# V times probabilities: column-tiled float32 pairs become full-array float32r matmuls of split parts

## The chip, the core and the metric

The kernel runs on one core of one Trainium2 chip. TensorE (PE) does the matrix products, and its weight loads stand in the profile as an engine of their own (PEld). VectorE (DVE), ScalarE (ACT) and GpSimd (POOL) do the elementwise work; SyncE (SP) issues the DMA transfers. Products land in PSUM, which has eight banks of 512 float32 columns for 128 partitions. All else is in SBUF or DRAM. The metric is device time in microseconds of the whole program, the median of a few executions.

## The reference, cut to what matters

Two transformer layers work on 512 latent tokens (a grid 64 wide) and 256 context tokens of 1,024 features. Layer 0 mixes tokens by neighbourhood attention with 16 heads of 64. Layer 1 mixes them by sliding-window attention in blocks of 128 queries, with 16 query heads over 4 key/value heads. Latent queries take one softmax over local keys and all context keys:

```python
s = jnp.concatenate([s_loc, s_ctx, s_sink], axis=-1)
p = jax.nn.softmax(s, axis=-1).astype(v.dtype)
return (jnp.einsum('bkgqs,bskd->bqkgd', p[..., :3 * T], v_blk)
        + jnp.einsum('bkgqc,bckd->bqkgd', p[..., 3 * T:3 * T + C], vc))
```

Each token mixer is followed by an output projection and a squared-ReLU MLP with 4,096 hidden features. Everything is float32. The last line above, V times probabilities, is what the change rewrites.

## The kernel before, in words

**Precision.** Most products run as float32r, a float32 form that TensorE takes in one pass but that keeps fewer bits. To get float32 accuracy an operand x is split into xH (x cast to float32r) and xL (x minus xH, again float32r); `split` (line 203) does this with a cast on ACT and a subtraction on DVE or POOL. A projection is then the three products H·H, H·L, L·H. Scores stack [kH; kL] over the 128 rows of the array and take [qH; qH] and [qL; qL] as stationary operands (`scores`, line 551), so that two products give all four parts. V times P is the exception: it runs in plain float32, with V (128 keys x 64 features) stationary in one half of the array's columns. `mm_halves` (line 198) puts two such products of two key blocks side by side, each into one half of the partitions of its sum, and `merge` (line 562) adds the halves with a copy on ACT and an addition on DVE.

**A head.** For each block of 128 queries PE forms the scores, DVE adds bias or mask and finds the maximum (one custom instruction), ACT takes the exponential with its sum, DVE the reciprocal, and DVE or POOL scales P. PE transposes P by blocks of 128 x 128 into PSUM (`tr`, `trs`), `evac_pt` (line 556) copies them to SBUF, and `mm_halves` takes them as moving operand.

**Layer 0.** `head0` (line 577) is one head, `qkv0(p)` (line 473) the projection of a pair of heads. `weave` (line 351) emits the steps of the attention of pair p and the projection of pair p+1 at an even pace. In `qkv0`, `front` takes a token tile's sum out of PSUM, norms it and makes `nat`; `back` transposes `nat` one tile later. In the first pairs the products of the modulation vectors (`ada_pe`) run along.

**Layer 1.** `kv1` (line 1131) projects keys, values and the first four heads' queries. `Head1` (line 1212) is one head: `front` for scores and softmax, `back` for V times P of the head before it. `q1` (line 1197) projects the next four heads' queries alongside. A query block of the two inner ones has five key blocks; its scores lie in a bank of 512 columns and in 128 columns of bank 2, so DVE takes two custom instructions in a chain. The MLPs (`mlp`, line 852) come behind each attention.

**Banks.** `banks[0..7]` are eight arrays of one PSUM bank each. In layer 0 the scores use banks 0 and 1 (`p_sc`), transposes 2, 3 and 6 (`p_pt`), V times P bank 7 (`p_pv`), projections bank 4. At the start `ada01(q)` (line 773) forms modulation vectors for two feature tiles in bank q mod 2, and `qkv0(0)` sums into banks 2 to 7. In the MLP of layer 1 the first product uses banks 4, 5, 0, 1 and the second one 2, 3, 6, 7.

**What sets the order.** Each engine runs its instructions in one fixed order. A scheduler chooses that order at build time from the program's order and its own estimate of times, and puts in the semaphore waits, so that an order can change at places that the diff does not touch. Where an engine is named in `pin`, it keeps the order of the program; PE is pinned from the MLP of layer 0 to the end of `kv1`.

Of the kernel before, what the change touches and what calls it, by code (L numbers as in the profile page):

```python
# [9 lines left out]
F32 = mybir.dt.float32  # L10
# [21 lines left out]
# column and shape of the small inputs in their pack  # L32
# [4 lines left out]
class Ring:  # L37
    """Equal slots of an arena, handed out in turn."""
# [10 lines left out]
def build(nc, tc, a):  # L49
    """a: DRAM access patterns by name."""  # L50
    with ExitStack() as es:
        _build(nc, tc, a, es)


def _build(nc, tc, a, es):
    pin = set()

    def pinned(*names):
        """Adds to `pin`; returns what undoes it."""
        added = set(names) - pin  # L60
# [53 lines left out]
    banks = [psum.tile([128, 512], F32, name=f"pq{i}", tag=f"pq{i}")[:] for i in range(8)]  # L114
# [28 lines left out]
    # the small inputs, packed  # L143
# [21 lines left out]
    # silu(c), silu(c_ctx), padded to 32 columns  # L165
# [32 lines left out]
    def mm_halves(pairs, start=False, stop=False):  # L198
        """Two products [128 x 64] . mv at once, one into each half of the partitions of its sum."""
        for at, (out, st, mv) in zip((0, 64), pairs):  # L200
            pe.matmul(out[at : at + 64], st, mv, start=start, stop=stop, tile_position=(0, at))

    def split(H_, L_, x, eng=None):
        """x == H_ + L_, both of float32r."""
# [56 lines left out]
    def ada_pe(layer, kinds, ring, ps_of, depth):  # L261
        """Vectors of the six, for both streams; one step per k tile, whose load runs `depth` steps ahead."""
# [44 lines left out]
    class Stream:  # L307
        """Weights [128, 1024] in the order of their use: loads and splits run ahead of the products."""
# [5 lines left out]
        def fill(self, n):  # L314
            """Up to n splits beyond the ones taken."""
# [18 lines left out]
    def run(gen, n=None):  # L334
        """The next n steps of a generator, or all."""
# [15 lines left out]
    def weave(*gens):  # L351
        """Generators with their step counts, emitted at an even pace."""
# [9 lines left out]
    class Stats:  # L362
        """R = 1 / sqrt(mean of squares + eps) of n tokens, on every partition; one step per feature tile."""
# [22 lines left out]
    def modulate(h_of, R, A, sh, uH, uL, tmp, view=None, split_of=None, fs=range(KT)):  # L386
        """u = h * R * A + sh, split."""
# [23 lines left out]
    def bias_tables():  # L411
        """Relative position bias per head in DRAM: of the interior queries with the mask, of the edge queries."""
# [7 lines left out]
    raw = Ring(FA, FX, 768, 2)  # L420
    xr = Ring(FA, FX + 1536, 256, 2)
    Pr = Ring(FA, FX + 2048, 512, 6)
    otmp = fr(5120, 512)
    biasr = Ring(FA, FX + 5632, 768, 2)
    natr = Ring(FA, FX + 7168, 512, 3)
# [8 lines left out]
    def head_norm(x, sq, nh):  # L434
        """rstd per head of x [128, nh * 64]; sq is scratch. One Newton step after the table functions."""
# [11 lines left out]
    def dup_mult(nat, x, r, nh, eng=g):  # L447
        """nat[:, h, 2, 64] = x[:, h, 64] * r[:, h], twice."""
# [977 lines left out]
```

## Time and profile before

| | |
|---|---|
| median of 3 runs | 1726.14 us (1725.89 to 1730.58) |
| profiled execution, first to last instruction | 1729.3 us, granted TensorE clock 0.984 of full speed |
| PE busy | 1664.0 us, 96% |
| DVE busy | 1147.3 us, 66% |
| ACT busy | 808.3 us, 47% |
| POOL busy | 568.8 us, 33% |
| chain that ended last | 73% PE, 11% DVE, 6% POOL |

The stages by their place in the profiled execution: start 0 to 75 us, attention of layer 0 to 466 us, output projection and MLP of layer 0 to 1130 us, `kv1` to 1172 us, attention of layer 1 to 1346 us, output projection and MLP of layer 1 to the end. A group row gives: line, engine, operation, out<-in by the program's names, the shape, the count | busy us, mean ns of one | idle time before, and what ended it. A timeline row gives start, length, engine, operation and how many like instructions follow each other. `pq` is PSUM; `RA` and `FA` are arenas of SBUF; `R` is one more SBUF region that is handed out anew from stage to stage. Every line number is that of a helper (L74), so names and shapes tell the groups apart. `128*64` in front of a shape is a stationary operand of 128 rows and 64 columns. A matmul's length reaches into the next one, since matmuls are pipelined; what one costs in a stream is the distance from start to start. A float32 matmul stands as two records.

### The profile page before, as it was taken

What the parts mean: (1) busy time and instruction counts of PE and PEld (TensorE: products, weight loads), DVE (VectorE), ACT (ScalarE), POOL (GpSimd) and SP (SyncE); (2) the same over time, 40 slices, a digit from 0 to 9 for tenths busy, and PEclk for the clock granted to TensorE, in tenths of its full rate; (3) what the DMA queues carried; (4) which work ended last, traced back from release to release, by engine and by line L of the source; (5) the groups of instructions that cost most, each with busy time, mean ns of one, the idle gap of its engine ahead of it and who ended that gap; (6) DMA issues with size and microseconds to landing.
All of it is one profiled execution on the core that took longest, in us unless ns stands there. A gap on an engine that the chain in (4) does not pass through costs nothing.

```text
span 1729.3 us, 25192 instructions
## 1 busy us (share of the span) xinstructions
PE 1664.0 (96%) x9554; PEld 1367.6 (79%) x9554; DVE 1147.3 (66%) x2188; ACT 808.3 (47%) x1668; POOL 568.8 (33%) x377
## 2 busy tenths in 40 slices
PE   6899999999998999999999999899999999999999
PEld 3867788887787887888888888687766988888887
DVE  5866667777467655666565656888787775555554
ACT  3656666677445343434343313556676442222220
POOL 2211111112147755749184901366551040000000
PEclk8999999999998999999999999999999999999999
DMA  9554321113124233333233311110021243232201
GB/s 312 159 179 134 121 77 45 44 52 109 38 94 155 101 114 106 128 106 122 87 119 110 122 49 62 55 44 25 13 78 63 86 158 98 97 98 96 95 30 49
DMA packets 63514, 165.63 MB, mean 96 GB/s; under 512 B 6816, under 2 KB 24608, under 8 KB 63008
## 3 DMA queue, kind: packets, MB, share of 16 engines
q1 hardware_dynamic: 63392, 164.02, 28.8%
q8 instruction: 75, 1.23, 0.3%
q14 instruction: 47, 0.39, 0.1%
HBM read 159.79 MB, written 7.34 MB: 97 GB/s over the span
## 4 chain that ended last, share of the span: by engine, by line
PE 73%; DVE 11%; POOL 6%; issue 5%; ACT 3%; DMA 2%; SPq 0%; POOLq 0%; DVEq 0%; ACTq 0%
PE pq L74 73%; DVE FA L74 5%; DVE RA L74 4%; POOL R L74 3%; POOL FA L74 2%; DMA FA<-in_ada_w_dram 2%; DVE smalls L74 2%; ACT RA L74 1%; ACT FA L74 1%; DVE R L74 1%; ACT R L74 0%; SPq L74 0%; DMA FA<-in_w_dram 0%; POOL RA L74 0%; ACT smalls L74 0%
## 5 line engine op out<-in xcount | busy, mean ns | idle before, releaser
L74 PE MATMUL pq<-RA 128*128 128x512 f32 (+3 forms) x6784 | 1282.2, 344 | 32.4 <-DVE FA L74 13.6
L74 PEld LDWEIGHTS pq<-RA 128*128 128x128 f32 x6784 | 1092.6, 192 | 193.6 <-issue 20.1
L74 ACT CAST RA<-FA 128x1024 fp32r<-128x1024 f32 (+3 forms) x299 | 230.6, 795 | 395.0 <-PE pq L74 233.8
L74 DVE TENSOR_TENSOR RA<-FA,RA 128x1024 fp32r<-128x1024 f32 (+3 forms) x265 | 300.4, 1149 | 114.2 <-ACT RA L74 109.8
L74 DVE SCALAR_TENSOR_TENSOR FA<-pq,mods,FA 128x512 f32<-128x512 f32 (+1 forms) x413 | 266.3, 662 | 159.2 <-PE pq L74 157.7
L74 POOL TENSOR_TENSOR R<-R,FA 128x1024 f32<-128x1024 f32 x84 | 221.0, 2663 | 3.8 <-ACT FA L74 1.8
L74 POOL TENSOR_TENSOR FA<-FA,smalls 128x256 f32<-128x256 f32 (+1 forms) x108 | 94.8, 880 | 362.0 <-DVE smalls L74 319.4
L74 PE MATMUL pq<-RA,R 128*128 128x512 f32 (+1 forms) x870 | 177.3, 350 | 0.6 <-DVE FA L74 0.3
L74 PEld LDWEIGHTS pq<-RA,R 128*128 128x128 f32 x870 | 143.4, 188 | 25.5 <-DVE FA L74 1.2
L74 POOL TENSOR_TENSOR FA<-FA 128x256 f32<-128x256 f32 (+2 forms) x103 | 86.5, 854 | 192.4 <-ACT FA L74 178.3
L74 PEld LDWEIGHTS pq<-ident,FA 128*128 128x128 f32 x802 | 92.4, 141 | 65.9 <-issue 49.1
L74 PE MATMUL pq<-ident,FA 128*128 128x128 f32 x802 | 134.3, 282 | 8.5 <-DVE RA L74 5.3
L74 POOL TENSOR_SCALAR FA<-FA,s 128x1024 f32<-128x1024 f32 x24 | 79.6, 3318 | 156.1 <-DMA FA<-in_ada_w_dram 127.6
L74 PE MATMUL pq<-R 128*64 128x512 f32 (+2 forms) x448 | 116.2, 471 | 3.1 <-ACT R L74 1.8
L74 ACT COPY R<-pq 128x512 f32<-128x512 f32 (+3 forms) x200 | 91.3, 476 | 40.9 <-PE pq L74 40.0
L74 POOL TENSOR_TENSOR RA<-FA,RA 128x1024 fp32r<-128x1024 f32 (+2 forms) x34 | 70.3, 2083 | 109.8 <-ACT RA L74 100.7
L74 ACT ACTIVATE FA<-FA,smalls 128x512 f32<-128x512 f32 (+1 forms) x120 | 89.2, 744 | 35.9 <-DVE smalls L74 35.0
L74 ACT ACTIVATE FA<-FA,s 128x1024 f32<-128x1024 f32 x60 | 69.0, 1151 | 78.5 <-POOL FA L74 62.7
L74 DVE SCALAR_TENSOR_TENSOR FA<-pq,FA 128x512 f32<-128x512 f32 (+1 forms) x96 | 57.1, 595 | 64.5 <-ACT FA L74 64.3
L74 ACT COPY FA<-pq 128x256 f32<-128x256 f32 (+4 forms) x130 | 55.8, 429 | 76.8 <-PE pq L74 70.9
L74 ACT ACTIVATE FA<-pq 128x512 f32<-128x512 f32 (+1 forms) x96 | 49.8, 520 | 83.2 <-PE pq L74 83.2
L74 ACT ACTIVATE FA<-FA 128x256 f32<-128x256 f32 (+1 forms) x131 | 59.2, 457 | 42.0 <-DVE FA L74 32.9
(78 smaller groups left out, 985.2 us busy)
## 6 DMA issues: line engine op xcount, KB each, us to landing
FA<-in_w_dram SPq DMA_DIRECT2D x128, 512.0 KB, 3.7
FA<-in_ada_w_dram SPq DMA_DIRECT2D x80, 512.0 KB, 3.8
FA<-in_wqkv_dram SPq DMA_DIRECT2D x32, 384.0 KB, 3.6
FA<-in_wo_dram SPq DMA_DIRECT2D x16, 512.0 KB, 3.5
FA<-in_ada_w_dram SPq DMA_DIRECT2D x20, 256.0 KB, 7.6
FA<-in_wq_dram SPq DMA_DIRECT2D x8, 512.0 KB, 3.5
R<-in_ada_w_dram SPq DMA_DIRECT2D x12, 256.0 KB, 6.2
FA<-in_xT_dram SPq DMA_DIRECT2D x2, 1024.0 KB, 6.3
```

The lines of the kernel that those rows point to most:

```text
L74: i = f(*args, **kw)
```

## The change

1. **V is split.** `front` of `qkv0` copies the whole projected tile (384 columns) to SBUF on ACT, and POOL makes vH and vL from it; `kv_front` in layer 1 does it with ACT and DVE out of PSUM. V is stored as [vH | vL], 128 columns. In layer 0 the norm factor of k is now multiplied in by POOL, no longer by DVE.
2. **P is split.** `evac_pt` writes P's transpose as H (cast on ACT) and L (subtraction on DVE).
3. **The products.** `mm_halves` goes; `pv` does two full-array float32r products for a key block, [vH | vL] with H and with L. `merge` stays: the lower half of the sum is now vL's share. The products of a block come one step later than before, behind the next block's transposes. The sum of context queries moves from bank 7 to the transposes' banks.
4. **Keys.** `key_at` puts the context's keys first, so that context and local keys of a query block are reached by one access pattern of two runs (`two`). Scores become one product of 512 keys in place of two of 256. The mask and the bias tiles follow the new key order.
5. **A two-bank array.** Banks 1 and 2 are now one array of 1,024 columns (`wide`), still handed out as two banks. In layer 1 the inner blocks' 640 scores lie in it, and DVE takes them in one custom instruction; the outer blocks use bank 0 alone.
6. **Balance and room.** In layer 1 the scaling of P of block 1 moves from DVE to ACT. The buffers of P's transposes are 3 of 1,024 (were 5 of 512) in layer 0 and 4 of 1,024 (were 3 of 512) in layer 1. The first half of `wo0` uses other weight slots.

```diff
-    banks = [psum.tile([128, 512], F32, name=f"pq{i}", tag=f"pq{i}")[:] for i in range(8)]
+    wide = None
+    banks = []
+    for i in (0, 1, 3, 4, 5, 6, 7):
+        n = 1024 if i == 1 else 512
+        x = psum.tile([128, n], F32, name=f"pq{i}", tag=f"pq{i}")
+        banks += [x[:, o : o + 512] for o in range(0, n, 512)]
+        if i == 1:
+            wide = x
...
+    def two(x, at, n):
+        x = x[:, 0:n]
+        return type(x)(x.tensor, x.offset, [list(x.ap[0]), [at, 2], [1, n]])
+    key_at = lambda t: (t + 2) % 6 * 128
...
-            s.copy(x, ps[:, 0:256])
+            s.copy(x, ps)
             V = views0(p)[3]
-            s.copy(V[:, t], ps[:, 256:384].rearrange("p (h d) -> p h d", h=2))
+            xv = x[:, 256:384].rearrange("p (h d) -> p h d", h=2)
+            g.tensor_copy(V[:, t, :, 0:DH], xv)
+            g.tensor_tensor(out=V[:, t, :, DH:128], in0=xv, in1=V[:, t, :, 0:DH].bitcast(F32), op=ALU.subtract)
...
-            v.tensor_tensor(out=nat[:, 256:384].rearrange("p (h d) -> p h d", h=2), in0=x[:, 128:256]...
+            g.tensor_tensor(out=nat[:, 256:384].rearrange("p (h d) -> p h d", h=2), in0=x[:, 128:256]...
...
-    def evac_pt(ps, lo, hi, eng=s):
+    def evac_pt(ps, lo, hi):
         pt = PTr.next()
-        (v.tensor_copy if eng is v else s.copy)(pt[:, 0 : hi - lo], ps[:, lo:hi])
-        return pt
+        H_, L_ = pt[:, 0 : hi - lo], pt[:, 512 : 512 + hi - lo]
+        s.copy(H_, ps[:, lo:hi])
+        v.tensor_tensor(out=L_, in0=ps[:, lo:hi], in1=H_.bitcast(F32), op=ALU.subtract)
+        return H_, L_
+    def pv(out, V, pt, lo, hi, start=False, stop=False):
+        for i, x in enumerate(pt):
+            mm(out, V, x[:, lo:hi], start and i == 0, stop and i == 1)
...
-                scores(ps[:, 0:256], T1, T2, t * 128, K[:, (t - 1) * 128 : (t + 1) * 128])
-                scores(ps[:, 256:512], T1, T2, t * 128, Kc)
+                scores(ps, T1, T2, t * 128, two(K, key_at(t - 1), 256))
...
     def kv_front(ps, t):
-        s.copy(V1[:, t], ps[:, 256:512].rearrange("p (h d) -> p h d", h=4))
+        xv = ps[:, 256:512].rearrange("p (h d) -> p h d", h=4)
+        s.copy(V1[:, t, :, 0:DH], xv)
+        v.tensor_tensor(out=V1[:, t, :, DH:128], in0=xv, in1=V1[:, t, :, 0:DH].bitcast(F32), op=ALU.subtract)
...
+                ps = wide[:, 0:640] if inner else p_sc.next()
+                scores(ps[:, 0:512], T1, T2, q0, two(K, key_at(first), 256))
                 if inner:
-                    px = banks[2][:, 128 * (t - 1) : 128 * t]
-                    scores(px, T1, T2, q0, K[:, q0 + 128 : q0 + 256])
-                    n1 = small()
-                    v.tensor_tensor_reduce(out=P[t][:, 512:640], in0=px, in1=mask[:, 512:640], ...)
+                    scores(ps[:, 512:640], T1, T2, q0, K[:, key_at(t + 1) : key_at(t + 1) + 128])
...
+                        elif t == 1:
+                            s.activation(P[t], P[t], AF.Copy, scale=r)
```

How the instructions stand on an engine before and now, at three places. `ISA` is the custom instruction or the reading of its accumulator; the buffer numbers of the two builds differ: before, pq_69 to pq_76 are banks 0 to 7; now pq_69 is bank 0, pq_70 is banks 1 and 2 together, and pq_71 to pq_75 are banks 3 to 7.

PE at the start, before: the modulation products of feature tiles 2 and 3 (`ada01(1)`, pq_70) stand ahead of the first products of `qkv0(0)` (pq_71 and on).

```order
L74 MATMUL pq_69<-FA,s_97 32x128 x12
L74 MATMUL pq_70<-FA,s_97 32x128 x4
L74 MATMUL pq_69<-ident,FA 128x128
L74 MATMUL pq_70<-FA,s_97 32x128 x4
L74 MATMUL pq_70<-R_68,s_97 32x128 x20
L74 MATMUL pq_71<-RA 128x384
```

The same place now; in the rows that "..." leaves out stand the rest of the 24 products of feature tiles 0 and 1.

```order
L74 MATMUL pq_69<-FA,s_96 32x128 x12
L74 MATMUL pq_69<-ident,FA 128x128
L74 MATMUL pq_70<-RA 128x384
L74 MATMUL pq_71<-RA 128x384
...
L74 MATMUL pq_70<-FA,s_96 32x128 x8
L74 MATMUL pq_70<-R_68,s_96 32x128 x24
```

All 32 products of `ada01(1)`, in bank 1, now come behind the 24 products that write, among others, bank 2 of the same array.

DVE in layer 1, before: part of one head's work beside the projection of queries.

```order
L74 TENSOR_TENSOR RA<-pq_74,RA 128x4x128
L74 ISA FA,smalls<-pq_71,FA,nsink 128x128
L74 ISA smalls 128x1
L74 TENSOR_REDUCE smalls<-FA 128x4
L74 ISA FA,smalls<-pq_69,FA,smalls 128x512
L74 ISA smalls 128x1
L74 TENSOR_SCALAR smalls<-smalls 128x4
L74 COPY R_8893<-pq_75 128x512
```

DVE in layer 1 now, at a like place:

```order
L74 TENSOR_TENSOR RA<-pq_73,RA 128x384
L74 ISA FA,smalls<-pq_69,FA,nsink 128x512
L74 ISA smalls 128x1
L74 TENSOR_TENSOR RA<-pq_71,RA 128x512
L74 TENSOR_TENSOR RA<-pq_74,RA 128x512
L74 ISA FA,smalls<-pq_70,FA,nsink 128x640
L74 ISA smalls 128x1
L74 TENSOR_TENSOR FA<-pq_75,FA 64x512
```

The copy of one block out of five has become a subtraction for every block, and the chain of a 128-column and a 512-column custom instruction has become one of 640 columns.

PE in the MLP of layer 1, before: a hidden tile in bank 1 (pq_70), then the four output tiles in banks 2, 3, 6 and 7.

```order
L74 MATMUL pq_70<-RA 128x512 x24
L74 MATMUL pq_71<-RA 128x512 x6
L74 MATMUL pq_72<-RA 128x512 x6
L74 MATMUL pq_75<-RA 128x512 x6
L74 MATMUL pq_76<-RA 128x512 x6
L74 MATMUL pq_73<-RA 128x512 x8
```

The same place now:

```order
L74 MATMUL pq_70<-RA 128x512 x24
L74 MATMUL pq_71<-RA 128x512 x6
L74 MATMUL pq_74<-RA 128x512 x6
L74 MATMUL pq_75<-RA 128x512 x6
L74 MATMUL pq_72<-RA 128x512 x14
L74 MATMUL pq_71<-RA 128x512 x3
L74 MATMUL pq_70<-RA 128x512 x6
```

The output tile in bank 2 now stands 35 products behind the hidden tile in bank 1, with banks 3, 6, 7 and 4 ahead of it.

More of the change, by code (lines that the diff above doesn't have):

```diff
@@ L665, in head0 @@
                 tr(ps, c * 256 + t * 128, Pc, t * 256 + c * 128)
-        pt = evac_pt(ps, 0, 512)
-        po = p_pv.next()[:, 0:256]
-        mm_halves([(po, Vs(4 + c), pt[:, c * 256 : c * 256 + 256]) for c in range(2)], start=True, stop=True)
+        cc_ = evac_pt(ps, 0, 512)
+        pv(po[:, 192:448], Vs(2), hi, 0, 256)
+        pv(po[:, 320:512], Vs(3), hi, 256, 448, stop=True)
+        merge(OT_lat[:, p], po, i)
+        po = p_pt.next()[:, 0:256]
+        for c in range(2):
+            pv(po, Vs(4 + c), cc_, c * 256, c * 256 + 256, start=c == 0, stop=c == 1)
         merge(OT_ctx[:, p], po, i)
@@ L844, in _build @@
     p_pt = Banks(2,3)
-    Pr = Slots(*(fr(2048 + 512 * i, 512) for i in range(6)), *(fr(7168 + 512 * i, 512) for i in range(3)))
+    Pr = Slots(*(fr(2304 + 512 * i, 512) for i in range(6)), *(fr(7424 + 512 * i, 512) for i in range(2)))
     es = wo0.early(Banks(4,5,6), ((0,0),(1,0),(2,0)), range(7))
@@ L1288, in mid @@
                 trs(ps, 0, b, (b - 1, b, b + 1))
-                return po[:, (b - 1) * 128 : (b + 2) * 128], Vs(b), evac_pt(ps, 0, 384)[:, 0:384]
-            blocks = [ctx(0)]
+                pt = evac_pt(ps, 0, 384)
+                return lambda: pv(po[:, (b - 1) * 128 : (b + 2) * 128], Vs(b), pt, 0, 384, stop=b == 2)
+            late = ctx(0)
             yield
-            blocks.append(ctx(1))
-            yield
-            ee = ends()
-            mm_halves(blocks, start=True)
-            yield
-            blocks = [mid(1)]
-            mm_halves(ee)
-            yield
-            blocks.append(mid(2))
-            yield
-            mm_halves(blocks, stop=True)
+            for make, arg in ((ctx, (1,)), (ends, ()), (mid, (1,))):
+                x = make(*arg)
+                late()
+                late = x
+                yield
+            x = mid(2)
+            late()
+            x()
             merge(OT_lat[:, h // 2], po, h % 2)
```

139 lines of the change are left out of this document (67 added, 72 removed).

## Prediction

> **What bounds the kernel now.** I read the page first: busy shares, then the chain of work that ended last.
>
> ```profile
> span 1729.3 us, 25192 instructions
> PE 1664.0 (96%) x9554; PEld 1367.6 (79%) x9554; DVE 1147.3 (66%) x2188; ACT 808.3 (47%) x1668; POOL 568.8 (33%) x377
> PE 73%; DVE 11%; POOL 6%; issue 5%; ACT 3%; DMA 2%; SPq 0%; POOLq 0%; DVEq 0%; ACTq 0%
> ```
>
> PE is the bound on average, and 73% of the chain is PE. But the change touches the two attentions, so next comes the table of stretches. Its columns are the stretch, its length, then busy us with instruction count of PE, PEld, DVE, ACT and POOL, the granted clock, DMA share and GB/s. The first two rows are the attention of layer 0, the third is `kv1`, and the last four are the heads of layer 1 in fours.
>
> ```profile
> 100.00:316.00 216.00, 211.67 (x1362) 164.23 (x1363) 142.71 (x422) 137.97 (x390) 34.47 (x43) 0.99 0.31 100
> 316.00:426.00 110.00, 107.40 (x643) 87.28 (x641) 81.89 (x235) 81.45 (x231) 23.24 (x27) 1.00 0.21 64
> 1130.00:1172.00 42.00, 38.38 (x276) 36.20 (x275) 38.75 (x92) 22.58 (x60) 28.90 (x38) 0.92 0.13 45
> 1172.00:1222.00 50.00, 50.00 (x346) 37.53 (x345) 39.46 (x108) 34.71 (x86) 29.03 (x33) 1.00 0.10 33
> 1222.00:1273.00 51.00, 49.67 (x325) 35.91 (x323) 43.18 (x107) 36.50 (x88) 29.94 (x31) 1.00 0.11 37
> 1273.00:1309.00 36.00, 34.94 (x218) 22.81 (x216) 31.24 (x85) 27.68 (x66) 11.30 (x8) 1.00 0.15 52
> 1309.00:1346.00 37.00, 36.61 (x213) 24.91 (x214) 20.06 (x49) 19.21 (x44) 6.02 (x5) 1.00 0.19 65
> ```
>
> Layer 0 is PE's: DVE has 66% and 74%. In layer 1 DVE stands at 79%, 85%, 87% and 54%, and in `kv1` at 92%, above PE's 91%. So PE time that the change frees is worth its full length in layer 0, and much less in three quarters of layer 1, where the change also gives DVE more to do.
>
> **What the old products cost.** From the timeline of PE, a stretch with three groups of column-tiled products between transposes in layer 0, and one in layer 1. The mixed group of 192 and 256 columns is named by its first shape.
>
> ```profile
> 419.76 1.07 PE L74 MATMUL pq<-R 128*64 128x512 f32 x2
> 420.77 0.66 PE L74 MATMUL pq<-ident,FA 128*128 128x128 f32 x4
> 421.36 0.65 PE L74 MATMUL pq<-R 128*64 128x192 f32 x4
> 421.94 0.55 PE L74 MATMUL pq<-ident,FA 128*128 128x128 f32 x3
> 422.42 0.65 PE L74 MATMUL pq<-R 128*64 128x256 f32 x4
> 422.99 0.98 PE L74 MATMUL pq<-ident,FA 128*128 128x128 f32 x7
> ...
> 1304.40 0.87 PE L74 MATMUL pq<-R 128*64 128x384 f32 x4
> 1305.20 1.39 PE L74 MATMUL pq<-RA 128*128 128x256 f32 x10
> ```
>
> From start to start a pair takes 1.01 us at 512 columns, 0.58 and 0.57 at 192/256 and 256, 0.80 at 384. The transposes between them are slower than in a stream: four take 0.59 us and three 0.48, where a long run (below) has 0.12 each, so 0.48 and 0.36. That is 0.11 to 0.12 us that a change between 64-column and 128-column operands costs, per group: 1.13, 0.70, 0.69 and 0.92 us.
>
> **What the new ones cost.** Long runs of full-array float32r products with 512, 384 and 256 columns, and of transposes:
>
> ```profile
> 1549.66 7.19 PE L74 MATMUL pq<-RA 128*128 128x512 f32 x31
> ...
> 411.17 3.74 PE L74 MATMUL pq<-RA 128*128 128x384 f32 x20
> 414.75 0.27 PE L74 MATMUL pq<-ident,FA 128*128 128x128 f32 x1
> ...
> 464.87 4.09 PE L74 MATMUL pq<-RA 128*128 128x256 f32 x32
> 468.88 0.65 PE L74 MATMUL pq<-R 128*64 128x256 f32 x4
> ...
> 1306.42 1.64 PE L74 MATMUL pq<-ident,FA 128*128 128x128 f32 x12
> 1307.85 0.74 PE L74 MATMUL pq<-RA 128*128 128x256 f32 x4
> ```
>
> One product costs 0.23 us at 512 columns (7.19 / 31), 0.18 at 384 (3.58 / 20), 0.125 at 256 (4.01 / 32). A group of two key blocks is four of them: 0.92, 0.72 and 0.50 us; I price 192 like 256. The columns that stream are as many as before (two passes of a full array for four of half an array); the gain is the switching and the tail of each float32 pair. A head of layer 0 has groups of 512, 192/256, 256 and 256 columns: it saves 0.21 + 0.20 + 0.19 + 0.19 = 0.79 us. A head of layer 1 has 512, 256 and 384: 0.21 + 0.19 + 0.20 = 0.60. Scores: four products of 256 (0.50) become two of 512 (0.46), on three tiles in layer 0 and four in layer 1: 0.12 and 0.16. Together 0.91 and 0.76 us a head, 26.7 us for 16 heads each. That is the low end, since groups that wait longer today, and switches in front of float32r products, are not in it. The high end takes 4% less for each new product and twice the switch: 0.91 + 0.11 + 0.46 = 1.48 and 0.76 + 0.09 + 0.35 = 1.20, in all 43. I take 1.05 for layer 0, nearer the rows: 16.8 us.
>
> **What the new splits cost.** Groups by shape; the last row stands in the stretch 1270 to 1335 us of the same view, the one before it in 1180 to 1270.
>
> ```profile
> L74 DVE TENSOR_TENSOR RA<-pq,RA 128x512 fp32r<-128x512 f32 x16 | 10.8, 680 | 0.1
> L74 DVE TENSOR_TENSOR FA<-pq,FA 64x256 f32<-64x256 f32 x16 | 6.7, 421 | 8.5 <-ACT FA L74 8.2
> L74 DVE COPY R<-pq 128x512 f32<-128x512 f32 x16 | 11.0, 686 | 11.9 <-PE pq L74 11.8
> L74 DVE TENSOR_SCALAR FA<-FA,smalls 128x640 f32<-128x640 f32 x24 | 16.4, 708 | 0.0
> L74 DVE CUSTOM_DVE_ANT_0 FA<-pq,FA,nsink 128x128 f32<-128x128 f32 x24 | 8.2, 343 | 3.7 <-PE pq L74 3.6
> L74 DVE TENSOR_TENSOR FA<-FA,smalls 128x128 f32<-128x128 f32 x48 | 17.1, 359 | 1.3
> L74 ACT COPY R<-pq 128x512 f32<-128x512 f32 x80 | 45.1, 588 | 6.9 <-PE pq L74 6.4
> L74 POOL TENSOR_TENSOR FA<-FA 128x128 f32<-128x128 f32 x16 | 7.5, 490 | 12.3 <-PE pq L74 12.3
> L74 DVE TENSOR_TENSOR smalls<-smalls 128x4 f32<-128x4 f32 x15 | 5.7, 383 | 3.9 <-ACT smalls L74 3.9
> L74 DVE TENSOR_TENSOR smalls<-smalls 128x4 f32<-128x4 f32 x8 | 1.2, 156 | 0.4 <-ACT smalls L74 0.4
> ```
>
> The subtraction for P's L reads PSUM and writes float32r, which is the first row's form: 0.68 us at 512 columns; between it and 0.42 at 256 I put 0.63 at 448 and 0.55 at 384.
>
> Layer 0, DVE: five subtractions, 3 x 0.68 + 2 x 0.63 = 3.3 us a head, less three multiplications of k at 0.36 that go to POOL: +2.2 us. In the second stretch 110 us hold five heads, 22 us each, with 16.4 us of DVE; 18.6 us in 22 - 1.05 is 89%, and the first stretch stays lower. No more than DVE does in layer 1 today, so I let layer 0 keep its gain: **-16.8 us**. ACT copies as before; POOL's 18 new operations a pair, 0.5 us each, fall on an engine that is 16% to 21% busy.
>
> Layer 1, DVE: 3 x 0.68 + 2 x 0.55 = 3.1 us, less a copy (0.69), a scaling that goes to ACT (0.71), and two short custom instructions with their accumulator reads (0.85), plus 0.35 for two that grow from 512 to 640 columns: **+1.2 us** a head, 4.8 a group of four. The groups then hold 44.3, 48.0, 36.0 and 24.9 us of DVE. PE alone would give 47.0, 48.0, 33.0 and 34.0, and the middle two can't be had: with DVE at 90%, between the 87% of the third group and the 92% of `kv1`, they last 49.2, 53.3, 40.0 and 34.0 us, 176.5 for 174 now: **+2.5 us**. At 95% it is 168 (-6), at 85% 185 (+11). ACT gains a cast (0.59) and the scaling, about 1.3 us a head, and reaches at most 41.7 of 53.
>
> `kv1`: six subtractions for vL, 256 columns, 0.42 us each, on the engine that sets its pace: 2.5 us, of which I take **+2**; 0 if they fall in its idle 8%.
>
> The start: the order shows `ada01(1)` behind 24 products, where before it stood ahead.
>
> ```profile
> 27.90 0.66 PE L74 MATMUL pq<-R,s 128*32 128x128 f32 x8
> 28.49 4.99 PE L74 MATMUL pq<-RA 128*128 128x384 f32 x20
> 33.31 0.27 PE L74 MATMUL pq<-ident,R 128*128 128x128 f32 x1
> ...
> 35.48 0.79 PE L74 MATMUL pq<-RA 128*128 128x384 f32 x3 [1.11 <-ACT RA L74]
> ```
>
> The transpose at 33.31 opens the way to the second lot of products at 35.48. It now waits for 32 small products behind the 24, 4 x 0.59 us by the first row's distance to the second, less the 0.59 that stood there already: **+2 us**; 0 if later loads are late anyway, 3 if the SP queue, whose next loads wait for the slots of these products, runs dry. The first projection of pair 1 in bank 2 is pushed back likewise: **+1**. In layer 1's MLP the moved output tile has 35 products, 8 us, for cover: 0, and 2 if weights are then late.
>
> Sum: -16.8 + 2.5 + 2 + 2 + 1 = -9.3 us on the profiled 1729.3, so 1720.0. The profiled span lies 3.2 us over the median of the runs, 1726.14; with the same difference the forecast is **1717 us**.
>
> **Rivals.** *PE sets the pace everywhere.* The merged custom instruction and ACT's share shorten the softmax chain, DVE reaches 97%, and both layers keep PE's gain. For it: PE is 99% to 100% busy in layer 1's first group. Against: DVE's 36.0 us in a group that PE would end in 33. 16 x (1.05 + 0.90) = 31, less 5: 1700 us. Chance 0.17.
>
> *The shared port eats it.* The last two rows of the groups show one small DVE instruction with two SBUF inputs at 383 ns where POOL is busy 60% of the time, and at 156 where it is nearly idle. Layer 0 gains 48 tiles x 3 POOL operations. If each holds up one such instruction by 0.23 us, DVE takes 2.1 us a head more, 20.7 of 21: the second half of layer 0 would need 23 us a head at 90%, 1 us more than now, and the first gain is halved. About -4 in layer 0, +7.5 elsewhere: 1729 us. Against: the new subtractions read PSUM, and the 680 ns row stands in stretches with POOL busy. Chance 0.20. The Trainium skill, "SBUF — State Buffer", section Terms, states such a rule: DVE and GpSimd arbitrate for a pair of ports, and the loser is blocked for the whole instruction. By that rule the 383 ns are waiting, and the trace agrees.
>
> *The two-bank array ties the banks, and it is slower.* At the start the order keeps bank 1's products behind bank 2's, though they share nothing but the array. If reads and writes of both banks are held apart as if they were one, then in layer 0 each change between scores in bank 1 and transposes in bank 2, some five a head, waits for the other's readers: ACT 0.59 plus DVE 0.68, 1.27 us, 102 us in all. It decides from 10% of that left uncovered; a quarter, 25 us, gives 1742. For it: PE takes its queue in order. Against: the scheduler knows of these waits and puts projection products between. Chance 0.20.
>
> **How the numbers follow.** Forecast 0.43, with its own range 1707 to 1727; the rivals 0.17, 0.20 and 0.20. No change means within 0.3%, 1721 to 1731, about what a measurement of this kernel can tell. Faster: 0.7 of the forecast and the first rival, 0.47. Same: the rest of the forecast and 0.6 of the second, 0.25. Slower: the third and the rest, 0.28. The range 1698 to 1742 reaches to both outer rivals.
>
> **What would show it.** Column-tiled groups gone, and in 100 to 426 us heads about 1 us shorter: the saving is right. DVE near 90% in the middle groups of layer 1 with their length not under today's: DVE sets the pace there; PE at 100% and 47, 48, 33 us: the first rival. Small DVE instructions with two SBUF inputs longer in layer 0: the port. PE waiting for DVE or ACT ahead of writes to bank 1 or 2: the tie. I am wrong if layer 0 does not get shorter, or if layer 1 does by more than 6 us.

## The result, and the profile after

The changed kernel takes 1777.42 us (median of 4 runs, 1776.38 to 1783.77); the kernel before, on the same chip, 1726.02. The ratio is 1.0299 with a 95% interval of 1.0279 to 1.0319: 3% slower, 60 us over the forecast of 1717 and 35 above the range. Its page begins so (the span, PE's row, the chain by engine):

```profile
span 1775.4 us, 24909 instructions
PE 1643.2 (93%) x9330; PEld 1401.8 (79%) x9330; DVE 1190.6 (67%) x2210; ACT 828.9 (47%) x1652; POOL 636.4 (36%) x521
PE 60%; DVE 18%; POOL 6%; ACT 6%; issue 5%; DMA 4%; SPq 0%; DVEq 0%; POOLq 0%; ACTq 0%
```

PE has 21 us less to do and is idle for 132 us instead of 65. Its share of the chain falls from 73% to 60%, DVE's rises from 11% to 18%. So PE now waits, and the question is where. Four DVE instructions that both kernels have serve as marks: the first addition of `merge` in layer 0, the last one there, the first subtraction of `kv_back`, and the last addition of layer 1. From the timeline of DVE, of the kernel before and then of the changed one:

```profile
115.77 0.66 DVE L74 TENSOR_TENSOR FA<-pq,FA 64x512 f32<-64x512 f32 x1
470.04 0.43 DVE L74 TENSOR_TENSOR FA<-pq,FA 64x256 f32<-64x256 f32 x1 [2.29 <-ACT FA L74]
1121.40 0.69 DVE L74 TENSOR_TENSOR RA<-pq,RA 64x512 fp32r<-64x512 f32 x1 [0.32 <-ACT RA L74]
1345.64 0.69 DVE L74 TENSOR_TENSOR FA<-pq,FA 64x512 f32<-64x512 f32 x1 [8.03 <-ACT FA L74]
```

```profile
122.66 0.68 DVE L74 TENSOR_TENSOR FA<-pq,FA 64x512 f32<-64x512 f32 x1
506.56 0.43 DVE L74 TENSOR_TENSOR FA<-pq,FA 64x256 f32<-64x256 f32 x1 [0.49 <-ACT FA L74]
1172.16 0.69 DVE L74 TENSOR_TENSOR RA<-pq,RA 64x512 fp32r<-64x512 f32 x1 [5.61 <-ACT RA L74]
1390.92 0.69 DVE L74 TENSOR_TENSOR FA<-pq,FA 64x512 f32<-64x512 f32 x1 [3.41 <-ACT FA L74]
```

The start takes 6.9 us longer, the attention of layer 0 29.6 (383.9 for 354.3), the way from there to `kv1` 14.2, `kv1` with the attention of layer 1 5.5 less (218.8 for 224.2), and the rest 0.8 more. About 7 of the 14.2 are no loss of that stage: PE does 52 more products behind the mark (3,552 for 3,500), which before were done ahead of it, and is busy there for 635.1 us instead of 628.6. I therefore add the two stretches from now on: 1005.6 us before, 1049.5 now.

What PE waits for in the attention of layer 0, by the view of waits: first before (115.8 to 470.0 us), then after (122.7 to 506.6); the columns are total us, times, longest.

```profile
PE pq L74 <- DMA FA<-in_ada_w_dram: 3.0, 2, 2.0
PE pq L74 <- DVE RA L74: 2.3, 2, 1.3
PE pq L74 <- DVE smalls L74: 1.7, 3, 0.8
```

```profile
PE pq L74 <- DVE RA L74: 12.2, 10, 3.7
PE pq L74 <- DVE smalls L74: 10.0, 14, 1.7
PE pq L74 <- ACT FA L74: 5.4, 7, 1.4
```

`DVE smalls` is the custom instruction that reads a score's bank; `DVE RA` and `ACT FA` read transposes and sums. So the readers of transposes hold PE up at least as long as those of scores. The timeline of the changed kernel (PE, then DVE) shows one place where scores wait:

```profile
344.24 0.73 PE L74 MATMUL pq<-RA 128*128 128x512 f32 x2 [0.79 <-DVE smalls L74]
345.77 0.74 PE L74 MATMUL pq<-RA 128*128 128x256 f32 x4 [0.79 <-DVE smalls L74]
346.97 0.48 PE L74 MATMUL pq<-perm,FA 128*128 128x128 f32 x1 [0.46 <-POOL FA L74]
```

```profile
343.49 0.69 DVE L74 CUSTOM_DVE_ANT_0 FA<-pq,FA 128x512 f32<-128x512 f32 x1 [0.54 <-PE pq L74]
345.02 0.69 DVE L74 CUSTOM_DVE_ANT_0 FA<-pq,FA 128x512 f32<-128x512 f32 x1 [0.24 <-PE pq L74]
```

Scores, then DVE, then scores, then DVE: each waits for the other, although scores have two banks. The order of PE tells why; here pq_70 is the array of banks 1 and 2, and in brackets stands the engine that an instruction waits for:

```
L74 MATMUL pq_70<-RA 128x256 [waits DVE_49]
L74 MATMUL pq_70<-RA 128x256 x3
L74 MATMUL pq_73<-RA 128x512 [waits Activation_49]
L74 MATMUL pq_73<-RA 128x512 x5
L74 MATMUL pq_70<-RA 128x512 [waits DVE_49]
L74 MATMUL pq_70<-RA 128x512
L74 MATMUL pq_70<-RA 128x256 [waits DVE_49]
```

Three scores in a row go into bank 1, each behind the reader of the one before. Written A for bank 0 and B for bank 1, the scores of layer 0 run A B A A A B B B A B, over and over, in the changed kernel; before they ran A B A B A B. While transposes in bank 2 are unread, bank 1 can't be written; that the scheduler bunches the scores because it knows this is my reading, which no run tests.

### The profile page after: what moved, and what is told of

Same layout as the page of the kernel before. It is cut to its first block, busy times and chain, and to the rows that moved or that the text cites. A ratio compares the mean times of both kernels' runs of the same rounds, so it can differ in the third digit from the quotient of the medians.

```text
span 1775.4 us, 24909 instructions
## 1 busy us (share of the span) xinstructions
PE 1643.2 (93%) x9330; PEld 1401.8 (79%) x9330; DVE 1190.6 (67%) x2210; ACT 828.9 (47%) x1652; POOL 636.4 (36%) x521
## 4 chain that ended last, share of the span: by engine, by line
PE 60%; DVE 18%; POOL 6%; ACT 6%; issue 5%; DMA 4%; SPq 0%; DVEq 0%; POOLq 0%; ACTq 0%
PE pq L74 60%; DVE FA L74 8%; DVE RA L74 7%; POOL R L74 3%; ACT FA L74 3%; DMA FA<-in_ada_w_dram 3%; POOL FA L74 3%; DVE smalls L74 3%; ACT RA L74 2%; DVE R L74 1%; ACT R L74 0%; SPq L74 0%; DMA R<-in_ada_w_dram 0%; ACT smalls L74 0%; DMA FA<-in_wqkv_dram 0%
## 5 line engine op out<-in xcount | busy, mean ns | idle before, releaser
L74 PEld LDWEIGHTS pq<-RA 128*128 128x128 f32 x6560 | 1079.6, 192 | 222.8 <-DVE smalls L74 22.5
L74 PE MATMUL pq<-RA,R 128*128 128x512 f32 (+3 forms) x1232 | 276.8, 354 | 14.4 <-DVE RA L74 8.6
L74 PEld LDWEIGHTS pq<-RA,R 128*128 128x128 f32 x1232 | 203.4, 190 | 56.1 <-DVE RA L74 15.3
L74 POOL TENSOR_TENSOR FA<-FA,smalls 128x512 f32<-128x512 f32 (+2 forms) x156 | 128.6, 838 | 245.3 <-DVE smalls L74 190.8
L74 PE MATMUL pq<-ident,FA 128*128 128x128 f32 x802 | 141.4, 288 | 16.4 <-DVE RA L74 6.3
L74 PEld LDWEIGHTS pq<-ident,FA 128*128 128x128 f32 x802 | 103.0, 147 | 33.1 <-DVE RA L74 6.9
L74 DVE TENSOR_TENSOR RA<-pq,RA 128x512 fp32r<-128x512 f32 (+3 forms) x155 | 98.1, 647 | 37.7 <-ACT RA L74 36.3
L74 ACT ACTIVATE FA<-FA,smalls 128x512 f32<-128x512 f32 (+1 forms) x128 | 95.7, 749 | 45.7 <-DVE smalls L74 44.6
L74 ACT CAST RA<-pq 128x512 fp32r<-128x512 f32 (+2 forms) x155 | 83.2, 553 | 44.5 <-PE pq L74 43.2
L74 ACT COPY FA<-pq 128x384 f32<-128x384 f32 (+5 forms) x130 | 60.6, 468 | 45.6 <-PE pq L74 35.1
```

The source lines that it names most:

```text
L74: i = f(*args, **kw)
```

## The experiments

My theory was the third rival: the two-bank array ties banks 1 and 2. Against it stood the new splits, which lengthen the way from transposes to products, and the shared port. This table has each kernel's stretches between the marks in its one profiled execution (us), and its ratio to the kernel before on the same chip with the 95% interval. It also holds a warning: up to `kv1` PE's order is the same in e2, e4, e8 and e10, yet the mark there stands at 1112.3, 1101.8, 1107.2 and 1112.0. Differences under 10 us in one profile's first two columns show nothing. In the third column e8 and e9, with the same order of PE there, differ by almost 5, so less than 5 us shows nothing either.

| | start | layer 0 to `kv1` | `kv1`, attention 1 | rest | median | ratio |
|---|---|---|---|---|---|---|
| before | 115.8 | 1005.6 | 224.2 | 383.7 | 1726.02 | 1 |
| changed | 122.7 | 1049.5 | 218.8 | 384.5 | 1777.42 | 1.0299 (1.0279 to 1.0319) |
| e1 | 118.9 | 1059.1 | 240.9 | 384.6 | 1800.84 | 1.0433 (1.0403 to 1.0464) |
| e2 | 119.3 | 993.0 | 222.4 | 383.8 | 1715.19 | 0.9954 (0.9937 to 0.9971) |
| e3 | 119.1 | 993.9 | 223.0 | 383.8 | 1720.56 | 0.9976 (0.996 to 0.9992) |
| e4 | 116.4 | 985.4 | 224.8 | 383.4 | 1713.53 | 0.9918 (0.9902 to 0.9934) |
| e5 | 117.5 | 970.4 | 210.2 | 383.8 | 1684.90 | 0.9763 (0.9742 to 0.9784) |
| e6 | 118.0 | 1024.4 | 218.6 | 384.4 | 1746.41 | 1.0116 (1.0092 to 1.014) |
| e7 | 118.5 | 986.7 | 224.0 | 383.4 | 1710.35 | 0.9896 (0.9878 to 0.9915) |
| e8 | 119.2 | 988.0 | 224.3 | 383.4 | 1714.82 | 0.9939 (0.9921 to 0.9957) |
| e9 | 117.6 | 988.1 | 219.6 | 383.5 | 1714.59 | 0.9938 (0.9922 to 0.9954) |
| e10 | 119.2 | 992.8 | 228.1 | 383.7 | 1718.29 | 0.9962 (0.9949 to 0.9975) |
| e11 | 123.8 | 1012.8 | 225.0 | 383.8 | 1745.29 | 1.0102 (1.007 to 1.0134) |
| e12 | 120.2 | 1054.0 | 222.3 | 383.8 | 1782.40 | 1.0325 (1.0296 to 1.0355) |
| e13 | 118.3 | 991.8 | 219.9 | 383.7 | 1714.12 | 0.9933 (0.9918 to 0.9948) |
| e14 | 116.9 | 986.4 | 224.3 | 383.5 | 1711.06 | 0.9911 (0.9894 to 0.9928) |

### e1: the array alone

The edit, on the kernel before:

```diff
-    banks = [psum.tile([128, 512], F32, name=f"pq{i}", tag=f"pq{i}")[:] for i in range(8)]
...
+    for i in (0, 1, 3, 4, 5, 6, 7):
+        n = 1024 if i == 1 else 512
+        x = psum.tile([128, n], F32, name=f"pq{i}", tag=f"pq{i}")
+        banks += [x[:, o : o + 512] for o in range(0, n, 512)]
...
```

> The kernel before with one edit: banks 1 and 2 are one array of 1,024 columns; all products, splits and keys are the old ones. Theory A (the two-bank array ties banks 1 and 2: each waits for readers of the other): this alone makes the kernel before slower by 25 to 55 us, most of it in the attention of layer 0 (+20 to +40) and the rest in the output projection and MLP of layer 0 (+8 to +18). Theory B (the loss comes from the new V and P splits, which lengthen the way from transposes to products): 1726 us, within 5 us of the kernel before.

Measured: 4.3% slower, more than the whole change, and some 20 us beyond theory A's window. From layer 0 to `kv1` it loses 53.5 us, of which 43.1 in the attention of layer 0, and 16.7 in `kv1` and layer 1, where this kernel keeps scores in bank 1 and their fifth block in bank 2. That array alone, with the old products, makes the kernel slower than the changed one. Theory B's 1726 falls.

### e2: the change with eight arrays

```diff
+    banks = [psum.tile([128, 512], F32, name=f"pq{i}", tag=f"pq{i}")[:] for i in range(8)]
...
-                ps = wide[:, 0:640] if inner else p_sc.next()
-                scores(ps[:, 0:512], T1, T2, q0, two(K, key_at(first), 256))
+                ps = p_sc.next()
+                scores(ps, T1, T2, q0, two(K, key_at(first), 256))
...
                 if inner:
-                    scores(ps[:, 512:640], T1, T2, q0, K[:, key_at(t + 1) : key_at(t + 1) + 128])
+                    px = banks[2][:, 128 * (t - 1) : 128 * t]
+                    scores(px, T1, T2, q0, K[:, key_at(t + 1) : key_at(t + 1) + 128])
...
```

> The changed kernel with eight arrays of one bank each; the inner blocks' scores in layer 1 again lie in a bank of 512 columns and in 128 columns of bank 2, read by two custom instructions in a chain; all else as changed. Theory A (the tie): 1715 to 1735 us, 40 to 60 under the changed kernel; the attention of layer 0 loses its 30 extra us, while layer 1 gives back up to 10 for the second custom instruction. Theory B (the splits): 1765 to 1790 us, layer 0 as slow as in the changed kernel.

Measured: 1715.19 us, 0.5% faster than the kernel before. 56.5 us come back between layer 0 and `kv1`. The view of stretches sets the attention of layer 0 side by side: before, changed, e2.

```profile
115.80:470.00 354.20, 346.56 (x2144) 272.96 (x2145) 235.76 (x675) 228.66 (x638) 59.91 (x71) 0.99 0.26 83
```

```profile
122.70:506.60 383.90, 343.53 (x2040) 295.89 (x2041) 262.51 (x716) 231.40 (x606) 118.48 (x186) 0.93 0.25 76
```

```profile
119.30:462.60 343.30, 326.51 (x2045) 290.11 (x2042) 260.00 (x714) 227.17 (x604) 118.00 (x185) 0.97 0.28 85
```

For the same products the changed kernel's PE is idle for 40.4 us and e2's for 16.8, and it is busy 17 us longer, at a granted clock of 0.93 instead of 0.97. DVE, ACT and POOL do the same in both. So of the 40.6 us a good half is waiting, and the rest goes with a lower clock. The Trainium skill, "TensorE: Matmul & The Clock Gate", Part 1, says that the clock follows how busy PE has been lately; the two rows agree.

### e3: k on DVE again

```diff
-            g.tensor_tensor(out=nat[:, 256:384]...
+            v.tensor_tensor(out=nat[:, 256:384]...
```

> As e2_eight_banks, and in layer 0 the multiplication of k by its norm factor stands on DVE again, as in the kernel before. Port theory (POOL's new operations hold up DVE's small instructions): 5 to 15 us faster than e2_eight_banks, all of it in layer 0. Otherwise: DVE gets 1 us a head more to do (3 x 0.36) and the time is the same as e2_eight_banks within 3 us, or up to 5 us longer if DVE is near its bound.

Measured: 1720.56 for e2's 1715.19, 5 us longer if anything; the intervals overlap. The port theory wanted 5 to 15 less from this one of POOL's three new operations a tile, so its window falls; the other two, for vH and vL, stayed on POOL. Its sign in the trace is missing too. The small instruction with two SBUF inputs, at 316 to 416 us, by groups, before and after:

```profile
L74 DVE TENSOR_TENSOR smalls<-smalls 128x4 f32<-128x4 f32 x13 | 4.1, 315 | 0.1
```

```profile
L74 DVE TENSOR_TENSOR smalls<-smalls 128x4 f32<-128x4 f32 x12 | 3.3, 275 | 0.2
```

It became shorter, with POOL twice as busy over the stage (118.5 us for 59.9). In these 100 us of e2 it stands at 355 ns, so a short window decides little; over the whole attention of layer 0 it takes 295 ns before, 228 in the changed kernel and 248 in e2. The sign is missing there too.

### e4 and e8: one array in layer 1 only

e4 hands banks 1 and 2 out as two arrays, as one for the attention of layer 1, and as two again: `join(True)` closes both and opens one of 1,024 columns in their place, `join(False)` the reverse. e8 frees them earlier in `kv1`.

```diff
     kv1()
     unpin()
+    wide = join(True)
...
+    join(False)
     run(heads[15].back())
```

> The changed kernel, but banks 1 and 2 are two arrays of their own up to the end of kv1 and again behind the attention of layer 1; only for that attention they are handed out anew as one array of 1,024 columns. Theory A (the tie costs where its two banks change places often, and the 640-column custom instruction is a gain): start to kv1 as with eight banks, the attention of layer 1 as short as in the changed kernel (150 us between its marks, 159 with eight banks): 1703 to 1710 us, faster than the kernel before by 0.8% to 1.2%. Rival (layer 1 is short in the changed kernel only because work piled up ahead of it): layer 1 stays at 157 to 160 and the time at 1713 to 1718.

> As e4_join_in_layer_1, but kv1 uses banks 1 and 2 only for the two context tiles, which are read first (latent tiles and the first queries go to banks 0, 3, 4 and 5), so that the 1,024-column array can be handed out while kv1 still runs. From the first mark of kv1 to the last of layer 1's attention e4 took 224.8 us and the changed kernel, whose array needs no handing out, 218.8. If the late handing out costs that: 217 to 221 here, and 2 to 7 us less than e4 in all, 1705 to 1711. If not: within 2 us of e4 in that stretch.

Measured: 1713.53 and 1714.82, both faster than the kernel before; `kv1` with the attention of layer 1 takes 224.8 and 224.3. So neither the expected 218.8 nor the price of handing out late appeared, and e4's time lies in the window of its rival, not in 1703 to 1710. But layer 1 didn't stay at 157 to 160: from the first to the last addition it takes 152.6 and 154.0 us, for e2's 158.7. What is shorter there begins later: the first addition comes 72.2 and 70.3 us behind the mark of `kv1`, for e2's 63.7. In all, the 640-column instruction is no gain over two in a chain that these runs could show (e2: 222.4).

### e5: DVE's subtraction left out

```diff
         s.copy(H_, ps[:, lo:hi])
-        v.tensor_tensor(out=L_, in0=ps[:, lo:hi], in1=H_.bitcast(F32), op=ALU.subtract)
-        return H_, L_
+        return H_, H_
```

> As e4_join_in_layer_1, and DVE's subtraction for P's L is left out: the second product of each key block takes H again, so that PE does the same work and DVE 3.1 to 3.3 us a head less (P's low part is missing from the sum). If DVE sets the pace in layer 1 (the prediction's ground for counting no gain there): its attention gets 10 to 25 us shorter than in e4, layer 0 less than 5. If PE's work and the order of the steps set it: layer 1 within 4 us of e4. If the subtraction costs by lengthening the way from transposes to products: both layers get shorter, each by 5 to 15.

Measured: 1684.9, some 29 us less than e4: 14.9 from layer 0 to `kv1`, 14.5 in `kv1` and layer 1. The third reading was nearest. In layer 0, which I had given to PE alone, 3.3 us of DVE a head cost 0.93 us against e4, and 1.2 against the mean of the four kernels with e4's order there. Whether by DVE's time or by the longer way to the products, the edit can't tell, since it takes away both.

### e6: the tie elsewhere

```diff
-    p_mm, p_sc, p_pt, p_pv, p_ad = Banks(4), Banks(0, 1), Banks(2, 3, 6), Banks(7), Banks(0, 1)
+    p_mm, p_sc, p_pt, p_pv, p_ad = Banks(4), Banks(0, 1), Banks(5, 3, 6), Banks(7), Banks(0, 1)
```

What stood in bank 5 in layer 0 goes to bank 2.

> The changed kernel with its two-bank array, but in layer 0 banks 2 and 5 change roles: transposes of P go to banks 5, 3 and 6, while bank 2, the partner of the scores' bank 1, takes the sums of the modulation vectors and, late, the second projection. The array is the same, only its banks change places less often. Theory A (each change of places between the two banks waits for the other's readers): most of layer 0's 40 extra us go while bank 2 holds modulation sums only, some stay from pair 4 on; in all 1735 to 1760. Rival (the array costs by itself, for instance by its place in PSUM, whoever uses it): 1770 to 1785 as the changed kernel.

Measured: 1746.41, inside theory A's window. The same array costs 31 us less when its second bank holds sums that are written for long and read seldom. So its place alone doesn't set the price; which data share it does. That the number of changes of roles is what counts fits, but wasn't varied by itself, and another 31 us over e2 remain.

### e7: scores by 256 columns

```diff
-                scores(ps, T1, T2, t * 128, two(K, key_at(t - 1), 256))
+                scores(ps[:, 0:256], T1, T2, t * 128, Kc)
+                scores(ps[:, 256:512], T1, T2, t * 128, K[:, key_at(t - 1) : key_at(t - 1) + 256])
```

> As e4_join_in_layer_1, but the scores of 512 keys are again two products of 256 keys for each part, context and local keys, in both layers. The prediction counts 0.12 us a head in layer 0 and 0.16 in layer 1 for joining them, 4.5 us in all: 3 to 7 us slower than e4 if PE time is worth its length there, within 2 us of e4 if it is hidden behind DVE and ACT.

Measured: 1710.35 against e4's 1713.53, with intervals that overlap, and not 3 to 7 us more. Joining the scores gains nothing that can be seen; the 4.5 us of the sum weren't there.

### e9 and e10: DVE's share changed by little

```diff
-            if t == 0:
+            if t in (0, 2):
                 g.tensor_tensor(out=P, in0=P, in1=sm.broadcast_to([128, 512]), op=ALU.mult)
...
-                        elif t == 1:
-                            s.activation(P[t], P[t], AF.Copy, scale=r)
```

The first edit is e9's, the second e10's; each is made on e8.

> As e8_join_early, and in layer 0 POOL scales P of blocks 0 and 2 instead of block 0 alone: DVE 0.5 us a head less, POOL 1.08 more. Leaving out 3.3 us of subtractions a head made layer 0 16 us shorter, 0.3 us for each us of DVE, so 16 x 0.5 x 0.3 = 2.4 us less than e8 if DVE's busy time counts. If the time from scores to transposes counts, or POOL's hold on DVE: 0 to 6 us more than e8.

> As e8_join_early, and in layer 1 P of block 1 is scaled on DVE, as in the kernel before, instead of ACT: DVE gets 0.7 to 1.3 us a head more. If DVE sets the pace in the first three groups of layer 1 (94% to 96% busy there): its attention 8 to 14 us longer than in e8. If the order of the steps or PE sets it: within 4 us.

Measured: e9 1714.59, the same as e8, so its 2.4 us can't be told. e10 1718.29, 3.5 more. The stretch between the first and the last addition of layer 1, of e8 and e10:

```profile
1177.50:1331.50 154.00, 139.99 (x835) 116.73 (x834) 132.98 (x300) 120.63 (x274) 60.93 (x62) 0.96 0.13 44
```

```profile
1182.90:1340.10 157.20, 142.12 (x854) 116.20 (x853) 144.41 (x317) 112.84 (x263) 64.59 (x64) 0.99 0.13 43
```

DVE gets 11.4 us more to do and the stretch 3.2 longer. If DVE alone set the pace, it would have been 11. One profile can't carry a difference this small, but the medians, 3.5 us apart, say the same. By e5, 1 us of DVE work in these stages costs about 0.3 us; e10 and e3 fit that, though their intervals overlap those of e8 and e2.

### e11 and e12: a bank taken away

```diff
-    p_mm, p_sc, p_pt, p_pv, p_ad = Banks(4), Banks(0, 1), Banks(2, 3, 6), Banks(7), Banks(0, 1)
+    p_mm, p_sc, p_pt, p_pv, p_ad = Banks(4), Banks(0), Banks(2, 3, 6), Banks(7), Banks(0, 1)
+    p_mm, p_sc, p_pt, p_pv, p_ad = Banks(4), Banks(0, 1), Banks(3, 6), Banks(7), Banks(0, 1)
```

Both on e2: the first new line is e11, the second e12.

> As e2_eight_banks, but the scores of layer 0 have bank 0 alone; bank 1 lies idle there. In the changed kernel the order of PE puts scores into the same bank two or three times in a row, each waiting for DVE to have read the one before. Theory S (what the tie costs in layer 0 is this loss of the second score bank): layer 0 takes 370 to 395 us between its first and last mark, as in the changed kernel (384; 343 with eight banks), 1740 to 1765 in all. Theory W (it costs because transposes and scores wait for each other's readers, which one bank less does not bring): layer 0 stays under 360, 1710 to 1730 in all.

> As e2_eight_banks, but for the first seven pairs of heads in layer 0 P's transposes rotate through banks 3 and 6 only; bank 2 lies idle. If the tie costs what a missing transpose bank costs (theory T): layer 0 takes 370 to 395 us, 1740 to 1765 in all. If waits between transposes and scores are the price (theory W): layer 0 stays under 360, 1712 to 1735 in all.

Measured: between the marks of layer 0, e11 takes 362.6 us and e12 403.5, for e2's 343.3. The first and the last mark of e12, then PE's waits there:

```profile
120.15 0.68 DVE L74 TENSOR_TENSOR FA<-pq,FA 64x512 f32<-64x512 f32 x1
523.68 0.43 DVE L74 TENSOR_TENSOR FA<-pq,FA 64x256 f32<-64x256 f32 x1 [0.49 <-ACT FA L74]
```

```profile
PE pq L74 <- DVE RA L74: 18.5, 20, 2.9
PE pq L74 <- DMA FA<-in_ada_w_dram: 13.1, 10, 2.9
PE pq L74 <- ACT RA L74: 9.9, 8, 2.6
```

e11's time lies in theory S's window, its layer 0 in neither; e12 is above T's. In layer 0's attention a score bank costs 19 us, half of the 41 that the tie does, a transpose bank 60, more than the tie. The tie thus lies between the loss of one and of the other. How much of it is the bunching of scores and how much the transposes' waits stays open.

### e13 and e14: a bank more

```diff
             run(ad)
-            p_mm = Banks(4, 5)
+            if p == 4:
+                p_pt = p_tr = Banks(2, 3, 6, 5)
+                p_sc = Banks(0, 1, 5)
```

Both on e4: the line with `p_pt` is e13's, the one with `p_sc` e14's.

> As e4_join_in_layer_1, but from pair 4 to pair 6 in layer 0 (six heads) the transposes rotate through banks 2, 3, 6 and 5, and the projection of the next pair has bank 4 alone instead of 4 and 5. One transpose bank less over 14 heads cost 60 us, 4.3 a head. If the turn of the banks still limits layer 0 (theory T): a third of that comes back, 1.4 us a head, 8 to 10 us, 1702 to 1706. If three banks are enough and PE and DVE set the pace: within 3 us of e4; up to 6 us more if the projection misses its second bank.

> As e4_join_in_layer_1, but from pair 4 to pair 6 in layer 0 the scores rotate through banks 0, 1 and 5, and the projection of the next pair has bank 4 alone. One score bank less over 16 heads cost 19 us, 1.2 a head. If the turn of the scores' banks still limits layer 0: 2 to 4 us less than e4. If not: within 3 us; up to 6 us more if the projection misses its second bank.

Measured: 1714.12 and 1711.06, within 3 us of e4. A fourth transpose bank or a third score bank, lent by the projection for six heads, gives nothing that shows; the projection had one bank less for it, and the runs don't part the two. One less is dear. e4, e7, e8, e9, e13 and e14 beat both kernels, by 0.6% to 1% over the one before.

## Why the prediction was wrong

**The step that failed** is the cover of the third rival: the sum gives the two-bank array +3 us at the start and nothing in the attention of layer 0. I had found the mechanism (the tie at the start of the order) and its price, 102 us in all of layer 0, and wrote that it decides from 10% uncovered. Against it I set that "the scheduler knows of these waits and puts projection products between". A quarter uncovered gave 1742 at a chance of 0.20. No row carried that quarter. e2 shows 40.6 us in the attention of layer 0, 40% of the 102, and e1 and e2 show 53 to 57 us up to the mark of `kv1`. The order of the changed kernel puts scores into the same bank in a row, and PE waits 14 times for a score's reader, 10.0 us in all, beside 12.2 for `DVE RA`; PE's idle time there is 40.4 us for e2's 16.8. The order of the changed kernel could be read ahead of the run: the bunched scores stood in it, and I looked for the tie only at the start.

**Without the tie the sum was about right.** -9.3 us was forecast, or -12.3 without the tie's +3 at the start. e2 is at -0.46%, 8 us, and e8, the change with the one array in layer 1 alone, at -0.61%, 10.5. That is in good part luck, as the terms show.

**The start**: +2 for `ada01(1)` and +1 for pair 1. The first mark came 6.9 us late. The timeline of PE in the changed kernel shows the first products, the transpose that was said to wait, and the second lot of products:

```profile
26.64 7.08 PE L74 MATMUL pq<-RA 128*128 128x384 f32 x24 [8.52 <-ACT RA L74]
36.63 0.33 PE L74 MATMUL pq<-ident,R 128*128 128x128 f32 x1
39.94 1.68 PE L74 MATMUL pq<-RA 128*128 128x384 f32 x8 [1.43 <-ACT RA L74]
```

The transpose comes 3.3 us later than before and the second lot 4.5: the mechanism was right. In e1 and e6, with the same order at this place, the transpose comes 2.6 and 2.0 us later, so +2 was a fair price. The 6.9 at the mark is no measure of the tie: with it e1 and e6 are 3.1 and 2.2 late, and without it e2 is 3.5 late and e4, with e2's order, 0.6.

**Layer 0, -16.8**: e2, e4, e8 and e10, with the same order there, are 12.6, 20.2, 17.6 and 12.8 us below the kernel before from layer 0 to `kv1`, 15.8 in the mean. The size held by luck, its ground didn't: "layer 0 keeps its gain" though DVE gets 2.2 us a head more (1.8 by the stretches above). e5 shows that DVE's subtractions cost 0.9 to 1.2 us a head there. It also lies 35.2 us below the kernel before, so the gain beside them is 2.2 us a head, above my high end of 1.48. Two errors cancelled. In neither did joined scores have a part (e7).

The gain was larger because the old products cost more than I read. A float32 matmul stands as two records, so a row with two records is one product, not a pair. These are the two 512-column products of one head, and then a pair that does stand side by side, in the kernel before:

```profile
416.79 1.07 PE L74 MATMUL pq<-R 128*64 128x512 f32 x2
419.76 1.07 PE L74 MATMUL pq<-R 128*64 128x512 f32 x2
461.52 1.08 PE L74 MATMUL pq<-R 128*64 128x512 f32 x4
```

A product alone takes as long as the pair. In the attention of layer 0, 20 of the 32 products of 512 columns stand alone, 10 run into the next group and only 2 form a pair. So 15 of 16 heads paid 1.9 to 2.0 us where I priced 1.01. That this is the whole of the larger gain isn't shown.

**Layer 1, +2.5, and `kv1`, +2**: the changed kernel takes 5.5 us less there instead of 4.5 more, while e2, e4 and e8 lie within 2 us of the kernel before. The changed kernel's stretches by groups of four heads; the last three run between the additions of heads 3, 7, 11 and 15, and the first begins at a place of my choice:

```profile
1228.00:1271.80 43.80, 43.10 (x314) 39.88 (x313) 40.05 (x94) 33.55 (x82) 22.57 (x28) 1.00 0.07 24
1271.80:1315.00 43.20, 38.03 (x224) 31.04 (x223) 40.40 (x99) 38.78 (x89) 27.16 (x28) 0.96 0.12 38
1315.00:1352.30 37.30, 32.94 (x193) 25.52 (x191) 35.85 (x83) 33.33 (x75) 11.93 (x11) 1.00 0.18 57
1352.30:1391.00 38.70, 35.19 (x209) 29.84 (x209) 27.81 (x55) 24.83 (x54) 7.33 (x5) 1.00 0.19 62
```

DVE is at 94% and 96% in the middle groups, where I had capped it at 90% (at 95% my sum is 169, not 168), and its work there is 40.4 and 35.9 us, not 48.0 and 36.0. (The 48.0 came from a stretch of 51 us, which held more than four heads; from addition to addition the kernel before took 48.2 us with 40.4 of DVE.) Between the first and last addition of the layer it grew from 122.0 to 132.0 us, 0.66 a head instead of 1.2. One mis-sized term is the scaling that moved to ACT: I took it off at 0.71 us, but that of odd heads took more. In the groups before, the second row is block 1 of the odd heads, the first one the other inner blocks:

```profile
L74 DVE TENSOR_SCALAR FA<-FA,smalls 128x640 f32<-128x640 f32 x22 | 14.7, 691 | 0.0
L74 DVE TENSOR_SCALAR R<-R,smalls 128x640 f32<-128x640 f32 x8 | 7.7, 962 | 0.0
```

That makes about 0.1 of the missing 0.5 us; the rest isn't taken apart. `kv1` alone, from its mark to DVE's first custom instruction of layer 1, went from 39.2 us (at 1160.6) to 37.0 (at 1209.1). So the +2 for vL doesn't show there, and no run isolates vL.

**MLP of layer 1, 0**: 0.8 more, so right.

**The rivals**: PE pacing everywhere didn't come, since DVE's work costs about 0.3 us for each us (e5). For the shared port no run shows a cost: e3 gains nothing, and the small instruction got shorter. The tie was it.

## What to carry to other kernels

Where two buffers that change hands often become views of one array, look in the new order at who writes them next to whom, in every stage that uses them and not only in the one for which they were joined. Price a new wait by its place in the order: where two writers of one tie stand side by side, as in the rows above, PE waited 0.79 us and nothing covered it. And hand the array out for one stage at most, given back afterwards: here that turned 3% slower into 0.6% to 0.8% faster. No array at all gave 0.5% (e2), so that the one stage needed it isn't shown.

## What the runs showed of the hardware

The chip doesn't ask for the tie: the waits stand in the program's order, and e2 does without them. The Trainium skill, "PSUM — Partial Sum Buffer", section on bank collisions, asks for a guard by bank, and by it these two need none between them. New to me was how steep the supply of banks is in this kernel: one transpose bank less costs 60 us (e12), while one more, lent for six heads, gives nothing that shows (e13). In layer 0 PE that waits more also runs slower: 0.93 of the clock with 40.4 us idle in the changed kernel, 0.97 with 16.8 in e2, 0.99 with 7.6 before. And a float32 product on half the array's columns takes as long alone as two side by side: 1.07 and 1.08 us at 512 columns.
